# Who issues the small transfers: rotary swaps and key copies move from ScalarE's DMA queue to SyncE's

## The chip, the cores and the metric

The kernel runs on one core of one Trainium2 chip. The metric is device time in microseconds (us), from a median of three runs. A core has a matrix engine (TensorE, PE in the profile), two elementwise engines (VectorE, DVE; ScalarE, ACT), GpSimd (POOL) and SyncE (SP), which computes nothing and only issues transfers. ScalarE can issue transfers too. Every engine works through its own instructions strictly in order: an instruction that waits holds back everything written behind it on that engine.

## What is computed

Two layers of a decoder trunk on 512 tokens of width 1024. The change is in layer 0, the attention layer; the rest (two squared-ReLU MLPs and an RWKV-7 layer) is untouched. Cut to what matters:

```python
proj = h @ w_in                      # one combined projection: aq, ak, av, bq, bk, bv
def partial_rope(t, pos):            # rotates the first 16 of each head's 64 dims
    t1, t2 = tf[..., :8], tf[..., 8:16]
    return concatenate([t1*cos - t2*sin, t2*cos + t1*sin, tf[..., 16:]])
oa = mixture_of_dilations(partial_rope(aq)*scale, partial_rope(ak), av)          # 8 heads
ob = differential_attention(partial_rope(bq)*scale, partial_rope(bk), bv, lam)   # 4 heads, two maps each
return concatenate([oa, ob]) @ w_out
```

## The kernel before

All data are float32; a product is made of three matmuls on float32r halves: a tile x is split into a high part (a cast on ScalarE) and a low part (x minus the high part, on VectorE). Weights come in chunks of 256 rows by 512 columns, 512 KB each: one transfer issued by SyncE into `wraw` (three buffers), the cast `whi` on ScalarE (line 179), the rest `wlo` on VectorE (line 181). One chunk costs TensorE 24 matmuls.

`gemm_stream` (line 226) runs five projections one behind another, four chunks each: Qa (queries of the first mixer), Qka (its keys), Qb, Qkb (the same of the second mixer), Vb; then the output projection. All five share four PSUM banks. In the last chunk of a Q or K projection each bank is finished in turn, and `evac` (line 489) empties it: ScalarE copies it to `qraw` (line 493, two buffers), VectorE multiplies it by cos (line 494), and four small transfers of 8 partitions by 512 elements build the swapped rows in `sw` (lines 496 and 497, three buffers); GpSimd multiplies `sw` by sin into `rt` (line 499), and three pieces of the stream later VectorE adds `rt` (line 500). The next projection's first matmul into a bank waits until line 494 has read it. A third `qraw` waits until the transfers of the first have landed.

Beside the stream runs the attention itself. `stacked` (line 505) prepares one pair of heads: `qs` on ScalarE and VectorE, `kh` on ScalarE, `kl` on VectorE, each for one half of the partitions; two transfers of 64 by 512 elements copy `kh` and `kl` to the other half (lines 515 and 517). For each block of 128 queries TensorE makes scores, VectorE adds the mask (line 535), ScalarE takes the exponential (line 538), TensorE transposes it, ScalarE copies the transpose to `pts` (line 547), and TensorE multiplies it by V into `o`. So `pts` stands on ScalarE in the same line as the weight casts, the `qraw` copies and, before the change, the issues of the small transfers.

The order of the attention steps and the stream's pieces is written out by slots (`FILL`, line 112) and is fixed on TensorE: each TensorE instruction is bound behind the one before it. On the other engines a scheduler sets the order when the program is built; transfers are instructions of their issuing engine there.

Of the kernel before, what the change touches and what calls it, by code (L numbers as in the profile page):

```python
# [10 lines left out]
F32 = mybir.dt.float32  # L11
# [145 lines left out]
class Builder:  # L157
# [252 lines left out]
    def attention_layer(self):  # L410
        tc, nc, A = self.tc, self.nc, self.A
        with ExitStack() as ctx:
# [73 lines left out]
            def project_qk(c0, name):  # L486
                q = [ac.tile([P, S], F32, tag=f"Q{name}{m}", name=self.nm("Q" + name)) for m in range(4)]

                def evac(m, ps):
                    raw = aw.tile([P, S], F32, tag="qraw", name=self.nm("qraw"), bufs=2)  # L490
                    sw = swp[state["sw"] % 3]
                    state["sw"] += 1
                    nc.scalar.copy(raw, ps)
                    nc.vector.tensor_tensor(q[m], ps, cos, op=ALU.mult)  # L494
                    for o in (0, HD):
                        nc.scalar.dma_start(sw[o:o + 8], raw[o + 8:o + 16])
                        nc.scalar.dma_start(sw[o + 8:o + 16], raw[o:o + 8])
                    t = aw.tile([P, S], F32, tag="rt", name=self.nm("rt"))
                    nc.gpsimd.tensor_tensor(t, sw, sin, op=ALU.mult)
                    soon.append((count["pieces"] + 3, lambda: nc.vector.tensor_tensor(q[m], q[m], t, op=ALU.add)))  # L500
                return q, dict(w=W, row0=0, nk=KT, c0=c0, x=(xh, xl), evac=evac)
# [3 lines left out]
            def stacked(q, k):  # L505


                maps = []
                for hh in range(2):
                    own, other = SIDES[hh], SIDES[1 - hh]  # L510
                    qs, kh, kl = (aw.tile([P, S], F32R, tag=f"{n}{hh}", name=self.nm(n)) for n in ("qs", "kh", "kl"))
                    nc.scalar.activation(qs[own], q[own], AF.Copy, scale=-0.125)
                    nc.vector.scalar_tensor_tensor(qs[other], q[own], -0.125, qs[own], op0=ALU.mult, op1=ALU.subtract)
                    nc.scalar.copy(kh[own], k[own])
                    nc.scalar.dma_start(kh[other].bitcast(F32), kh[own].bitcast(F32))
                    nc.vector.tensor_tensor(kl[own], k[own], kh[own], op=ALU.subtract)
                    nc.scalar.dma_start(kl[other].bitcast(F32), kl[own].bitcast(F32))
                    maps.append((qs, kh, kl))
                return maps

# [84 lines left out]
            def steps_a(q, k, v, oh, ol, slot0):  # L605
                for m in range(4):
                    u = {}

                    def prepare(m=m):
                        prepared["a", m] = stacked(q[m], k[m])  # L610
# [29 lines left out]
            def steps_b(q, k, v, oh, ol, slot0):  # L640
                for h in range(4):
                    u, first = {}, slot0 + 4 * h

                    def prepare(h=h):
                        prepared["b", h] = stacked(q[h], k[h])
# [66 lines left out]
            plain, nc = nc, InOrder(self, ["tensor"])  # L712
# [25 lines left out]
            nc = self.nc = plain  # L738
# [1011 lines left out]
```

## Time and profile before

| | before |
|---|---|
| median of 3 runs (lowest, highest) | 1522.94 us (1520.53, 1524.39) |
| the profiled execution's own time | 1522.35 us |
| its span, first to last instruction | 1520.5 us |
| TensorE busy | 1427.7 us (94%) |
| VectorE busy | 889.8 us (59%) |
| ScalarE busy | 701.7 us (46%) |
| GpSimd busy | 351.6 us (23%) |
| mean granted TensorE clock | 0.972 |
| DMA queue of SyncE (q1): packets, MB | 103240, 140.37 |
| DMA queue of ScalarE (q10): packets, MB | 16320, 22.03 |

Times in the rows below count from the span's start. Issuing a transfer is not counted as busy time of an engine; it stands in the trace as a row of its own (ACTq, SPq), and its duration is how long that engine's instruction stream was held, not how long the data took. A number in square brackets at a row's end is how long the engine stood idle before it, and what released it. The granted clock is given as a share of full speed: 1.00 is 2.4 GHz, 0.50 is 1.2 GHz. The attention layer ends about 284 us into the span.

### The profile page before, as it was taken

How to read it: one execution, taken by the hardware profiler on the slowest of the kernel's cores; microseconds unless marked ns; L12 is line 12 of the kernel's file. 1: busy time of each engine (PE TensorE's matmuls, PEld its weight loads, DVE VectorE, ACT ScalarE, POOL GpSimd, SP SyncE). 2: the span in 40 equal slices, each digit the busy share in tenths (PEclk: the TensorE clock that was granted, in tenths of full speed). 3: DMA queues.
4: the chain of work that ended last, by engine and by line, in shares of the span. 5: the costliest groups of instructions: out<-in, count | busy, mean ns of one | idle time of the engine just before them, and what ended most of it. 6: DMA issues, size and time to landing. Idle time of an engine off the chain costs nothing. (4 is left out here: it accounts for less than half of the span.)

```text
span 1520.5 us, 24493 instructions
## 1 busy us (share of the span) xinstructions
PE 1427.7 (94%) x9506; PEld 1180.4 (78%) x9506; DVE 889.8 (59%) x1531; ACT 701.7 (46%) x1426; POOL 351.6 (23%) x368
## 2 busy tenths in 40 slices
PE   8988899999999999979888999989999999999998
PEld 6776687878888888857667788867787888888887
DVE  5545568833335464497866778878866333454543
ACT  4335576532234343336634666666655233343533
POOL 5111100300000010052345455546655000000100
PEclk9999999999999999979989999989999999999999
DMA  5242222333333343225554445444224333323331
GB/s 198 77 118 81 58 79 77 82 97 97 96 97 97 97 125 97 100 56 167 172 193 138 118 137 161 123 140 119 65 95 125 85 97 97 96 97 97 97 97 70
DMA packets 119676, 163.97 MB, mean 108 GB/s; under 512 B 23036, under 2 KB 58404, under 8 KB 119560
## 3 DMA queue, kind: packets, MB, share of 16 engines
q1 hardware_dynamic: 103240, 140.37, 31.0%
q10 hardware_dynamic: 16320, 22.03, 4.5%
q8 instruction: 75, 1.23, 0.3%
q14 instruction: 41, 0.34, 0.1%
HBM read 133.00 MB, written 19.92 MB: 101 GB/s over the span
## 5 line engine op out<-in xcount | busy, mean ns | idle before, releaser
L181 DVE TENSOR_TENSOR wlo<-wraw,whi 128x1024 fp32r<-128x1024 f32 x172 | 221.0, 1285 | 245.0 <-ACT whi L179 244.9
L179 ACT CAST whi<-wraw 128x1024 fp32r<-128x1024 f32 x172 | 180.2, 1048 | 225.9 <-PE g L189 185.0
L190 PE MATMUL g<-xh,wlo 128*128 128x512 f32 x512 | 199.1, 390 | 0.7 <-DVE wlo L181 0.6
L188 PE MATMUL g<-xh,whi 128*128 128x512 f32 x512 | 199.4, 390 | 0.0
L189 PE MATMUL g<-xl,whi 128*128 128x512 f32 x512 | 199.3, 389 | 0.0
L188 PE MATMUL g<-mh,whi 128*128 128x512 f32 x512 | 199.2, 389 | 0.0
L189 PE MATMUL g<-ml,whi 128*128 128x512 f32 x512 | 199.2, 389 | 0.0
L190 PE MATMUL g<-mh,wlo 128*128 128x512 f32 x512 | 199.2, 389 | 0.0
L366 POOL TENSOR_TENSOR acc<-acc,sq 128x512 f32<-128x512 f32 x29 | 49.4, 1705 | 610.5 <-issue 436.6
L196 DVE TENSOR_TENSOR ml<-m,mh 128x512 fp32r<-128x512 f32 x128 | 87.9, 689 | 151.2 <-ACT mh L195 151.2
L195 ACT CAST mh<-m 128x512 fp32r<-128x512 f32 x128 | 78.8, 617 | 190.2 <-PE g L190 190.0
L190 PEld LDWEIGHTS g<-xh,wlo 128*128 128x128 f32 x512 | 96.1, 188 | 21.4 <-DVE wlo L181 1.6
L188 PEld LDWEIGHTS g<-mh,whi 128*128 128x128 f32 x512 | 96.1, 188 | 20.1
L189 PEld LDWEIGHTS g<-xl,whi 128*128 128x128 f32 x512 | 96.1, 188 | 19.8
L188 PEld LDWEIGHTS g<-xh,whi 128*128 128x128 f32 x512 | 96.1, 188 | 19.9 <-ACT rb L372 0.2
L189 PEld LDWEIGHTS g<-ml,whi 128*128 128x128 f32 x512 | 96.1, 188 | 19.9
L190 PEld LDWEIGHTS g<-mh,wlo 128*128 128x128 f32 x512 | 96.1, 188 | 19.9
L149 POOL TENSOR_TENSOR wlo<-wraw,whi 128x256 fp32r<-128x256 f32 x100 | 76.2, 765 | 122.7 <-ACT whi L149 119.7
L806 POOL TENSOR_TENSOR xl<-mt,xh 128x512 fp32r<-128x512 f32 x28 | 50.1, 1803 | 84.0 <-ACT xh L804 77.4
L149 PE MATMUL side<-whi,xh 128*128 128x256 f32 x192 | 63.4, 330 | 0.0
L149 PE MATMUL g<-xh,whi 128*128 128x512 f32 x128 | 52.3, 409 | 8.2 <-DVE Qka L494 4.4
L188 PE MATMUL g<-whi,xh 128*128 128x512 f32 x128 | 51.6, 418 | 6.0 <-ACT xh L804 4.7
(331 smaller groups left out, 3079.8 us busy)
## 6 DMA issues: line engine op xcount, KB each, us to landing
wraw<-in_mlp_w_dram SPq DMA_DIRECT2D x128, 512.0 KB
wraw<-in_attn_w_in_dram SPq DMA_DIRECT2D x24, 512.0 KB
wraw<-in_rwkv_w_o_dram SPq DMA_DIRECT2D x16, 512.0 KB
wraw<-in_attn_w_out_dram SPq DMA_DIRECT2D x8, 512.0 KB
wraw<-in_rwkv_w_k_dram SPq DMA_DIRECT2D x8, 512.0 KB
wraw<-in_rwkv_w_r_dram SPq DMA_DIRECT2D x8, 512.0 KB
wraw<-in_rwkv_w_v_dram SPq DMA_DIRECT2D x8, 512.0 KB
xt<-in_x_dram ACTq DMA_DIRECT2D x4, 512.0 KB
```

The source lines that it names most:

```text
L149: ins = op(*args, **kw)
L179: ins = [nc.scalar.copy(hi, raw)]
L181: ins.append((eng or nc.vector).tensor_tensor(lo, raw, hi, op=ALU.subtract))
L188: mm(ps, lh, rh, start=start, stop=False)
L189: mm(ps, lh, rl, start=False, stop=False)
L190: mm(ps, ll, rh, start=False, stop=stop)
L195: nc.scalar.copy(hi, src)
L196: nc.vector.tensor_tensor(lo, src, hi, op=ALU.subtract)
L366: nc.gpsimd.tensor_tensor(self.acc[0], self.acc[0], sq, op=ALU.add)
L806: eng.tensor_tensor(xl[k], t, xh[k], op=ALU.subtract)
```

## The change

All four swap transfers of each rotary evacuation (16 evacuations, 64 transfers) and both copies in each half of `stacked` (32 transfers) are issued by SyncE. Nothing else in the source changes: no tile, no buffer count, no slot.

```diff
                     nc.vector.tensor_tensor(q[m], ps, cos, op=ALU.mult)
                     for o in (0, HD):
-                        nc.scalar.dma_start(sw[o:o + 8], raw[o + 8:o + 16])
-                        nc.scalar.dma_start(sw[o + 8:o + 16], raw[o:o + 8])
+                        nc.sync.dma_start(sw[o:o + 8], raw[o + 8:o + 16])
+                        nc.sync.dma_start(sw[o + 8:o + 16], raw[o:o + 8])
...
                     nc.scalar.copy(kh[own], k[own])
-                    nc.scalar.dma_start(kh[other].bitcast(F32), kh[own].bitcast(F32))
+                    nc.sync.dma_start(kh[other].bitcast(F32), kh[own].bitcast(F32))
                     nc.vector.tensor_tensor(kl[own], k[own], kh[own], op=ALU.subtract)
-                    nc.scalar.dma_start(kl[other].bitcast(F32), kl[own].bitcast(F32))
+                    nc.sync.dma_start(kl[other].bitcast(F32), kl[own].bitcast(F32))
```

TensorE's and GpSimd's order stays as it was, row for row; ScalarE's, VectorE's and SyncE's change. Three places:

ScalarE, the last evacuation of Qb (`qraw_1060`); minus is before, plus is now, and the numbers behind the names tell tiles apart:

```order
 L538 ACTIVATE sb_1050,sums_887<-sb_1050,mn_1051 128x256
+L179 CAST whi_1072<-wraw_1070 128x1024
+L547 COPY pts_1093<-t_1091 128x128
 L493 COPY qraw_1060<-g_793 128x512
-L179 CAST whi_1072<-wraw_1070 128x1024
-L496 DMA sw_419<-qraw_1060 8x512
-L497 DMA sw_419<-qraw_1060 8x512
-L496 DMA sw_419<-qraw_1060 8x512
-L497 DMA sw_419<-qraw_1060 8x512
-L547 COPY pts_1093<-t_1091 128x128
 L538 ACTIVATE sb_1098,sums_887<-sb_1098,mn_1099 128x384
```

The copy `pts_1093` stood behind the `qraw` copy, a cast and four issues; now it stands ahead of that `qraw` copy, behind the cast alone.

ScalarE, the last evacuation of Qkb (`qraw_1487`) up to the next `pts` that TensorE wants (`pts_1562`), before:

```order
L493 COPY qraw_1487<-g_1079 128x512
L538 ACTIVATE sb_1505,sums_1378<-sb_1505,mn_1506 128x512
L496 DMA sw_417<-qraw_1487 8x512
L497 DMA sw_417<-qraw_1487 8x512
L496 DMA sw_417<-qraw_1487 8x512
L497 DMA sw_417<-qraw_1487 8x512
L179 CAST whi_1511<-wraw_1509 128x1024
L195 CAST oh_814<-oc_1526 128x512
L547 COPY pts_1562<-t_1558 128x384
```

and now:

```order
L179 CAST whi_1511<-wraw_1509 128x1024
L493 COPY qraw_1471<-g_1078 128x512
L547 COPY pts_1500<-t_1497 128x256
L538 ACTIVATE sb_1505,sums_1378<-sb_1505,mn_1506 128x512
L512 ACTIVATE qs_1798<-Qb_442 64x512
L195 CAST oh_814<-oc_1526 128x512
L514 CAST kh_1799<-Qkb_446 64x512
L493 COPY qraw_1487<-g_1079 128x512
L547 COPY pts_1562<-t_1558 128x384
```

The issues are gone from in front of `pts_1562`; the `qs` and `kh` of the next head pair, which stood behind it, have moved ahead of it, and the weight cast `whi_1511` ahead of the third `qraw` copy.

SyncE, the end of the train of Qka's swaps (sixteen rows, of which the last two stand here) and what is now queued behind it; before, the two weight loads followed directly on the one ahead of the train:

```order
+L496 DMA sw_418<-qraw_774 8x512
+L497 DMA sw_418<-qraw_774 8x512
+L515 DMA kh_822<-kh_822 64x512
+L517 DMA kl_823<-kl_823 64x512
+L515 DMA kh_831<-kh_831 64x512
+L517 DMA kl_832<-kl_832 64x512
 L177 DMA wraw_875<-in_attn_w_in_dram 128x2x512
 L177 DMA wraw_931<-in_attn_w_in_dram 128x2x512
```

The weight loads `wraw_875` (Qb's last chunk) and `wraw_931` now wait behind sixteen swaps and four copies. At Qa's train the load `wraw_685` stands behind sixteen swaps in the same way; at Qb's and Qkb's the next loads do too.

## Rows read from the trace of the kernel before

**Rows 1.** Who TensorE waited for, first 430 us: total, times, longest, us

```profile
PE o L149 <- ACT pts L547: 10.1, 5, 4.6
PE g L149 <- DVE Qka L494: 4.4, 2, 2.4
PE g L149 <- DVE Qa L494: 3.7, 2, 2.0
```

**Rows 2.** Stretches: length, busy us (count) by engine, granted clock, DMA share, GB/s

```profile
60.00:80.00 20.00, 16.25 (x60) 12.19 (x59) 14.90 (x14) 7.22 (x10) 5.15 (x4) 0.83 0.25 69
80.00:100.00 20.00, 15.60 (x68) 12.26 (x67) 7.79 (x11) 5.22 (x8) 4.69 (x3) 1.00 0.34 99
120.00:140.00 20.00, 15.84 (x109) 11.81 (x108) 11.14 (x23) 11.01 (x25) 4.30 (x3) 0.83 0.24 61
160.00:185.00 25.00, 19.63 (x134) 15.14 (x133) 11.36 (x24) 10.37 (x26) 5.81 (x4) 0.86 0.24 67
```

**Rows 3.** Timeline of TensorE, the longest stall at Qb and two at Qkb: start, us

```profile
128.04 0.48 PE L149 MATMUL o<-Va,pts 128*64 128x64 f32 x4 [3.78 <-ACT pts L547]
...
162.75 0.69 PE L149 MATMUL o<-Va,pts 128*64 128x64 f32 x16 [0.76 <-ACT pts L547]
...
175.85 0.91 PE L149 MATMUL o<-Va,pts 128*64 128x64 f32 x12 [4.61 <-ACT pts L547]
```

**Rows 4.** Timeline of ScalarE, end of Qb's and of Qkb's last swap issues

```profile
127.04 0.63 ACTq L497 DMA_DIRECT2D sw<-qraw  x1
127.72 0.27 ACT L547 COPY pts<-t 128x128 f32<-128x128 f32 x1 [1.81 <-issue]
...
173.89 1.04 ACT L179 CAST whi<-wraw 128x1024 fp32r<-128x1024 f32 x1 [2.03 <-issue]
...
175.32 0.48 ACT L547 COPY pts<-t 128x384 f32<-128x384 f32 x1
```

**Rows 5.** Stretches of the evacuations of Qb and of Qkb, columns as in Rows 2

```profile
112.50:128.10 15.60, 10.88 (x88) 8.12 (x87) 8.71 (x17) 6.44 (x18) 3.83 (x3) 0.98 0.19 51
158.60:175.90 17.30, 11.93 (x94) 9.10 (x93) 8.54 (x18) 7.17 (x17) 4.39 (x4) 0.98 0.24 62
```

**Rows 6.** Timeline of ScalarE and VectorE at Qa's evacuation

```profile
67.74 0.58 ACT L493 COPY qraw<-g 128x512 f32<-128x512 f32 x1 [2.54 <-issue]
...
61.70 2.23 DVE L181 TENSOR_TENSOR wlo<-wraw,whi 128x1024 fp32r<-128x1024 f32 x1 [0.26 <-ACT whi L179]
...
64.46 0.68 DVE L494 TENSOR_TENSOR Qa<-g,cos 128x512 f32<-128x512 f32 x1
```

**Rows 7.** Timeline at Qka: ScalarE's first swap issue, VectorE's third and fourth cos product

```profile
85.47 0.63 ACTq L496 DMA_DIRECT2D sw<-qraw  x1
...
92.78 0.68 DVE L494 TENSOR_TENSOR Qka<-g,cos 128x512 f32<-128x512 f32 x1
...
96.89 0.69 DVE L494 TENSOR_TENSOR Qka<-g,cos 128x512 f32<-128x512 f32 x1
```

**Rows 8.** Issues by line: duration ns min/median/max, first and last start

```profile
L496 ACTq DMA_DIRECT2D sw<-qraw x32: 631/632/1260, 56.8 to 172.6; - x32
L515 ACTq DMA_DIRECT2D kh<-kh x16: 468/468/553, 95.8 to 240.5; - x16
L1125 SPq DMA_DIRECT2D kb<-kt x16: 472/483/1117, 794.5 to 1086.5; - x16
```

**Rows 9.** Weight loads: issues of SyncE, one load's DMA share, casts on ScalarE

```profile
75.00 0.37 SPq L177 DMA_DIRECT2D wraw<-in_attn_w_in_dram  x1
...
78.00:79.00 1.00, 1.00 (x6) 0.81 (x5) 0.14 (x1) 0.83 (x1) 0.00 (x0) 1.00 0.13 47
...
80.11 5.81 SPq L177 DMA_DIRECT2D wraw<-in_attn_w_in_dram  x2
...
110.94 1.05 ACT L179 CAST whi<-wraw 128x1024 fp32r<-128x1024 f32 x1 [0.55 <-PE g L149]
```

**Rows 10.** Timeline of GpSimd, the first product with the swapped rows

```profile
61.55 1.29 POOL L499 TENSOR_TENSOR rt<-sw,sin 128x512 f32<-128x512 f32 x1 [27.97 <-DVE Qa L494]
```

## The prediction

> **What bounds the kernel now.** TensorE is busy 94% of the span, so I first asked where it is not, and who ends that idle time. The view of who waited for whom, cut to the first 430 us and to TensorE, names three rows that matter here [rows 1]: 10.1 us in five waits for `pts` copies of ScalarE, 4.4 us in two waits for the cos product of Qka, 3.7 us in two waits for that of Qa. Together 18.2 us. The table by stretches places them: TensorE is busy 16.25, 15.60 and 15.84 of 20 us in the stretches from 60, 80 and 120 us, and 19.63 of 25 us from 160 [rows 2]. These are the last chunks of Qa, Qka, Qb and Qkb, the four times when banks are evacuated and swaps are issued. I call them places 1 to 4.
>
> The same table shows a second cost. The granted clock is 0.83 from 60 to 80, 0.83 from 120 to 140 and 0.86 from 160 to 185 [rows 2]. A mean of 0.83 over 20 us is 6.8 us at half speed (1.2 instead of 2.4 GHz), that is 3.4 us of lost work; place 4 loses 25 x 0.14 = 3.5 us. Place 2 stalls for 4.4 us in two pieces and keeps a clock of 1.00 [rows 1, 2], so not each stall pays it.
>
> Then the timelines. TensorE's two longest waits are 3.78 us, ended at 128.04, and 4.61 us, ended at 175.85, both by `pts` [rows 3]. On ScalarE the copy at 127.72 starts as soon as the last of four swap issues, 127.04 + 0.63, is over; ScalarE stood idle 1.81 us for "issue". At place 4 the weight cast follows at 173.89 after 2.03 us of "issue", and `pts` only at 175.32 [rows 4]. From 112.5 to 128.1 ScalarE computes 6.44 us of 15.6, from 158.6 to 175.9 it computes 7.17 of 17.3 [rows 5]: it is not short of time to compute, its stream is held by issuing. That is the wait which ends last at places 3 and 4.
>
> At places 1 and 2 it is a mixture: the wait is for VectorE's cos product, which follows ScalarE's `qraw`. The fourth `qraw` of Qa starts at 67.74 after 2.54 us of "issue", but the third cos product (64.46) follows VectorE's own work, among it a weight low part that took 2.23 us from 61.70 [rows 6].
>
> **The change part by part.** *What it removes from ScalarE.* 64 swap issues of 0.632 us and 32 copy issues of 0.468 us [rows 8]: 40.4 + 15.0 = 55 us of held instruction stream. Only the part that ends a wait of TensorE counts, so the sum is made by place, out of the waits and the clock.
>
> *Place 3.* Its waits for `pts` are the 10.1 us less place 4's 4.61 and 0.76 [rows 1, 3]: 4.7 us, of which 3.78 in one. In the new order four issues are gone from in front of each `pts`; `pts_1093` has one cast ahead of it instead of a copy, a cast and four issues. Four issues are 4 x 0.63 and gaps, 2.7 us, and the issues of the tiles before had delayed ScalarE already. With 6.44 us of computing in 15.6 [rows 5] each `pts` should be ready before TensorE, with 10.88 us of work, asks. Gain between 2.7 (one tile's issues alone) and 4.7; I take 4.3.
>
> *Place 4.* Waits of 4.61 and 0.76 [rows 3], 5.4 us. Here the new order is less kind: ahead of `pts_1562` now stand `qs` and `kh` of the next heads, and the `kh` cast needs the first Qkb tile with its `rt` added, hence its swaps landed. The two that moved ahead cost ScalarE about 1.2 us (half-tile operations, about 0.6 each, as the whole-tile copy in Rows 6), and TensorE asks at 175.85 - 4.61 = 171.24, some 12 us after the first of those swaps. I expect a residue of 0.6 us. Gain between 2.7 and 5.4; I take 4.8.
>
> *Places 1 and 2.* VectorE's order up to the third cos product is unchanged, so the first wait at each stays nearly whole. For the fourth, the four issues ahead of `qraw` go, and two half-tile operations each on ScalarE and VectorE come in ahead (`qs` at place 1, `kh` and `kl` at place 2). At place 2 VectorE would go: third cos product until 92.78 + 0.68 [rows 7], two `kl` and one addition at about 0.7 each, fourth cos product at 95.6 instead of 96.89: gain 1.3 us. At place 1 the same count from 64.46 + 0.68 gives 67.3, or 68.7 if the `qs` are stretched as the low part of 2.23 us was; now it follows the copy that ends at 68.32 [rows 6]: between a loss of 0.4 and a gain of 1.0, and I take 0.5.
>
> *The clock.* If the long stalls at places 3 and 4 go, the drops there should go: 3.4 and 3.5 us, less about 0.4 each for idle time that fell inside: 6 us for both. Place 1 keeps a stall of about 2 us, so I leave its clock as it is; its recovery would be worth 2.6 us more (3.4 less half of the second stall).
>
> *What it adds to SyncE.* The trace has no swap issued by SyncE. The nearest row is a transfer inside SBUF of the RWKV layer, `kb`, which SyncE issues in 0.483 us, where ScalarE needs 0.468 for the key copies [rows 8]: the price hardly depends on the engine, so I take 0.63 and 0.04 of gap for a swap; its ends are 0.63 and 1.26, the longest swap issue. SyncE's stream is in order too, and queued behind a swap that waits for its `qraw` are weight loads, for which TensorE would wait. A load lands about 3.6 us after its issue (issued at 75.00, the DMA share is down to 0.13 from 78 to 79) [rows 9]; the cast of 1.05 us [rows 9] and a low part of 1.2 to 2.2 us follow. Place 1: the train starts at 56.8 [rows 8] and goes out as the four copies come, until about 69. `wraw_685` behind it is Qka's last chunk, which TensorE begins some 2 us ahead of Qka's first swap at 85.47 [rows 7], so at about 83; ready by 69 + 3.6 + 2.3 = 75, it has 8 us to spare. Place 2: the train starts at 85.5, the fourth `qraw` comes at about 94, its swaps end at 97, four copies at 0.47 end at 99. `wraw_875`, issued at 85.5 now (the second of the two from 80.11 on [rows 9]), would go out at 99 and be ready by 105 to 107; TensorE turns to it when the chunk ahead of it ends, at 110.94 [rows 9] less the 1.8 us gained so far. It is hidden by 2 us or more. At places 3 and 4 attention is interleaved, a chunk takes longer, and the loads have more. Cost taken: 0; ends 0 and 5 us (at 1.26 us for a swap the train ends 9 us later and `wraw_875` comes up to 5 us late). The key copies' own move gains nothing: none of TensorE's waits in Rows 1 is for them, and their data are used several us later.
>
> A page of the Trainium skill speaks against the change. Perfetto Trace Analysis, section DMA Optimizations, advises balancing transfers over the engines that can issue them where generating descriptors is the bottleneck; the change gathers them on one. By that rule SyncE would be the next to be late, about 1545 as in the second rival; by Rows 8 and 9 its stream has room, 1505.
>
> *The sum.* 0.5 + 1.3 + 4.3 + 4.8 + 6 = 16.9 us. The profiled execution took 1522.35, which gives 1505.4; it lies 0.6 below the median of the three runs, which I neglect. Forecast 1505.
>
> **The rivals.** *Half of it comes back* (1513). One of places 3 and 4 keeps its long wait since the new order on ScalarE puts something that itself waits in front of `pts`: at place 4 `kh`, which waits for swaps, GpSimd and VectorE; at place 3 the cast `whi_1072`, which waits for TensorE's chunk to end. Price: one of the two gains, about 4.5 + 3 = 7.5 us. For it speaks that both stand so in the new order; against it that the swaps' data have some 10 us to arrive.
>
> *SyncE's train is slow* (1545). A swap may hold SyncE not 0.67 us but about 2, as long as one takes to land: the first four issues at Qa begin at 56.8 and end near 60.1 (one of 1.26, three of 0.67), and GpSimd starts on their data at 61.55 [rows 8, 10], 2.1 us after the last began; and in the new order nearly each swap waits for the landing of the transfer eight before. A train then lasts 32 us. At place 1 it ends at 89 and `wraw_685` is ready at 95, 12 us late; at place 2 the same count gives 125, 14 us late, and the `qraw` that wait for landings eat the gains at places 3 and 4: 1522 + 26 = 1548, about 1545 with some gain left. It begins to cost from about 0.95 us for a swap, where place 2's load just gets late, and makes the kernel slower than before from about 1.6. Against it: eight transfers back is 5 us back, and a swap lands in 2.
>
> *Nothing* (1522). What ScalarE spends on issuing is not what holds `pts`, or the same waiting appears on VectorE. Against it: 1.81 and 2.03 us of "issue" right ahead of the two late steps [rows 4]. DMA: Bandwidth & Descriptors of the Trainium skill, section Issuing engines are not separate DMA queues, says that using several engines only saves the sequencer's time to issue, "which is usually small relative to the DMA itself". Were it small here, moving it would change nothing; the trace does not agree, since 2.7 us of issuing for a tile stand against 2.1 us from an issue to its data.
>
> *More* (below 1499). Place 1's stall shrinks under what brings the clock down, since no weight load now runs beside the first swaps: 2.6 us, and the first stalls at places 1 and 2 lose another 1 to 2 us each.
>
> **How the numbers follow.** Forecast 0.58 (1499 to 1510), half back 0.17 (1510 to 1516), more 0.08, nothing 0.09 (1518 to 1527), slow train 0.08. Leaving out "nothing", "slow train" and the far end of "more" (0.03) leaves 0.80: range 1497 to 1517. What a measurement here can tell from no change is 0.3%, 4.6 us: faster 0.58 + 0.17 + 0.08 = 0.83, same 0.09, slower 0.08.
>
> **What would show it.** Right: TensorE's waits for `pts` fall from 10.1 us to under 2; those for Qka fall by about 1, those for Qa hardly; the clock is 1.00 from 100 to 200 us; the attention layer ends about 17 us earlier and nothing else moves beyond the clock's own play. SyncE's swaps last about 0.63 us. Wrong: a wait of `whi` or `wlo` for a load of weights, swap issues on SyncE above 0.95 us, a `pts` that comes after a `kh` or `whi` that waited, or a clock that stays low at places 3 and 4 though their stalls are gone. Clock drops of the layers behind may fall elsewhere when everything ahead is shorter; a few us either way there would be no sign for or against any step.

## The result: 1504.2 us, and the profile after

The changed kernel takes 1504.2 us (median of 4 runs, 1503.35 to 1506.7) against 1523.12 (1520.53 to 1524.39) for the kernel before. The ratio is 0.988, 95% interval 0.986 to 0.990. Forecast was 1505 in a range of 1497 to 1517. The profiled execution took 1504.68 us where before's took 1522.35, 17.7 us less; the spans are 1502.9 and 1520.5.

First the same view as [rows 1], who TensorE waited for in the first 430 us (total, times, longest). Only the rows that matter here are shown:

```profile
PE g L149 <- DVE Qka L494: 3.1, 2, 1.7
PE g L149 <- DVE Qa L494: 2.7, 2, 1.9
PE s L149 <- DVE ol L199: 2.6, 2, 2.2
```

The row for `pts` is gone (10.1 us before); Qka fell from 4.4 to 3.1 and Qa from 3.7 to 2.7. Together 12.4 us less. The table by stretches, columns as in [rows 2]:

```profile
60.00:80.00 20.00, 17.30 (x64) 13.15 (x63) 10.89 (x13) 6.44 (x9) 6.54 (x4) 0.83 0.31 90
...
120.00:140.00 20.00, 20.00 (x153) 15.60 (x152) 13.06 (x27) 12.90 (x30) 3.37 (x3) 1.00 0.44 123
...
160.00:185.00 25.00, 25.00 (x201) 19.67 (x201) 16.30 (x36) 14.57 (x35) 3.16 (x2) 1.00 0.34 98
...
220.00:240.00 20.00, 17.57 (x93) 14.82 (x92) 16.20 (x53) 10.53 (x37) 1.01 (x1) 0.91 0.21 66
```

At places 3 and 4 (now in the stretches from 100 to 185) TensorE is busy all the time at a clock of 1.00. That gives back 20 x 0.17 = 3.4 and 25 x 0.14 = 3.5 us. Place 1 keeps its 0.83. And a low clock turned up in a stretch where before had none: 0.91 from 220 to 240, which costs 20 x 0.09 = 1.8 us. So by these means the clock gave 5.1 us, and with the 12.4 us of waits that is 17.5 of 17.7 us. The agreement is closer than the account deserves: a mean over a stretch also counts low clock while TensorE stands idle, which the waits count already. An estimate that takes, microsecond by microsecond, only the time that TensorE worked at the low level gives back 6.3 us at places 3 and 4 together, less 1.6 for the new drop and 0.5 for place 1: 4.2 us, and 12.4 + 4.2 = 16.6. That fits what the traces show at the last transposes of the attention layer, first before, then now:

```profile
277.43 0.66 PE L149 MATMUL oc<-ident,ob 128*128 128x128 f32 x4 [0.40 <-DVE ob L593]
260.71 0.66 PE L149 MATMUL oc<-ident,ob 128*128 128x128 f32 x4 [0.38 <-DVE ob L593]
```

They come 16.7 us earlier. The other 0.9 us of the span came in the layers behind, which the change does not touch; where, stays open.

Why `pts` no longer comes late is seen on ScalarE. These are the end of Qb's evacuation (place 3) and of Qkb's (place 4), to be held against [rows 4]:

```profile
117.18 1.05 ACT L179 CAST whi<-wraw 128x1024 fp32r<-128x1024 f32 x1
119.01 0.27 ACT L547 COPY pts<-t 128x128 f32<-128x128 f32 x1 [0.78 <-PE t L149]
...
157.25 0.62 ACT L512 ACTIVATE qs<-Qb 64x512 fp32r<-64x512 f32 x1
...
158.24 0.63 ACT L514 CAST kh<-Qkb 64x512 fp32r<-64x512 f32 x1
158.76 0.59 ACT L493 COPY qraw<-g 128x512 f32<-128x512 f32 x1
159.24 0.49 ACT L547 COPY pts<-t 128x384 f32<-128x384 f32 x1
```

The `pts` at 119.01 is `pts_1093`, the one at 159.24 `pts_1562`; before, they started at 127.72 and 175.32, with four issues shortly ahead of them. At 119.01 ScalarE waits 0.78 us for TensorE's transpose, so now ScalarE is the one that is early. At place 4 `qs`, `kh` and the last `qraw` stand in front of `pts` as the new order said, and none of them waited.

SyncE's side, issues by line as in [rows 8] (duration ns min/median/max, first and last start):

```profile
L497 SPq DMA_DIRECT2D sw<-qraw x32: 624/624/1272, 57.2 to 161.4; - x32
...
L515 SPq DMA_DIRECT2D kh<-kh x16: 461/467/588, 96.0 to 216.7; - x16
```

A swap holds SyncE 0.624 us where it held ScalarE 0.632. So the price of issuing did not change; it was moved from an engine with something urgent to do to one without. What queued behind the train at place 2 is seen on SyncE, and the next weight cast and scores on ScalarE and TensorE:

```profile
98.89 1.14 SPq L177 DMA_DIRECT2D wraw<-in_attn_w_in_dram  x2
...
104.53 1.04 ACT L179 CAST whi<-wraw 128x1024 fp32r<-128x1024 f32 x1
...
103.42 0.22 PE L149 MATMUL s<-kh,qs 128*128 128x128 f32 x1
```

The first of the two loads, `wraw_875`, went out at 98.9 us and its cast started at 104.53 without having waited for it; the scores at 103.42 had not waited for the key copies, which went out from 96.0 on.

### The profile page after: what moved, and what is told of

Same layout as the page of the kernel before. It is cut to its first block, busy times and chain, and to the rows that moved or that the text cites. A ratio compares the mean times of both kernels' runs of the same rounds, so it can differ in the third digit from the quotient of the medians.

```text
span 1502.9 us, 24530 instructions
## 1 busy us (share of the span) xinstructions
PE 1421.1 (95%) x9506; PEld 1174.4 (78%) x9506; DVE 890.4 (59%) x1531; ACT 703.0 (47%) x1426; POOL 351.1 (23%) x368
## 5 line engine op out<-in xcount | busy, mean ns | idle before, releaser
L149 PE MATMUL side<-wlo,xh 128*128 128x256 f32 x192 | 55.5, 289 | 1.8 <-POOL wlo L149 1.7
```

The lines of the kernel that those rows point to most:

```text
L149: ins = op(*args, **kw)
```

## Experiments

**Which transfers, and which places.** Four kernels undo the change in part.

Swaps alone on SyncE:

```diff
-                    nc.sync.dma_start(kh[other].bitcast(F32), kh[own].bitcast(F32))
+                    nc.scalar.dma_start(kh[other].bitcast(F32), kh[own].bitcast(F32))
...
-                    nc.sync.dma_start(kl[other].bitcast(F32), kl[own].bitcast(F32))
+                    nc.scalar.dma_start(kl[other].bitcast(F32), kl[own].bitcast(F32))
```

> The rotary swaps alone on SyncE, the key parts' copies back on ScalarE. The theory (the swaps' issues on ScalarE stood in front of pts and qraw; the copies end no wait of TensorE): the time of the changed kernel within 2 us, 1503 to 1506; waits of TensorE for pts stay gone, clock 1.00 from 100 to 200 us. Rival (the copies' issues carry part of the gain, 32 x 0.47 us = 15 us of ScalarE's stream): about 1510 or more, with waits for pts of 2 us or more back at the fourth place, where two copies stand near pts.

Measured: 1502.68 us, ratio to before 0.989 (0.986 to 0.992). The whole gain is there without the copies (0.3 us below the range expected).

Copies alone on SyncE (the swaps' two lines back on `nc.scalar`):

> The key parts' copies alone on SyncE, the swaps back on ScalarE. The theory: 1521 to 1524, as the kernel before, with waits for pts of about 10 us and the clock at 0.83 from 120 to 140 us. Rival (the copies carry part of the gain): 1515 or less, the waits for pts smaller by several us.

Measured: 1520.8 us against 1520.5 in the same comparison, ratio 1.000 (0.9985 to 1.0012). The copies give nothing, as predicted; TensorE's waits for `pts` are 9.9 us.

By place (this is the edit for places 3 and 4; the other run has `"a", "ka"` in it):

```diff
+                    queue = nc.sync if name in ("b", "kb") else nc.scalar
...
-                        nc.sync.dma_start(sw[o:o + 8], raw[o + 8:o + 16])
-                        nc.sync.dma_start(sw[o + 8:o + 16], raw[o:o + 8])
+                        queue.dma_start(sw[o:o + 8], raw[o + 8:o + 16])
+                        queue.dma_start(sw[o + 8:o + 16], raw[o:o + 8])
```

> Swaps of Qb and Qkb (places 3 and 4) on SyncE, those of Qa and Qka (places 1 and 2) on ScalarE; copies on SyncE. The theory: most of the gain, 10.1 us of stalls and 6 us of clock out of 18.9, so 1505 to 1508; waits for pts gone, those for Qa and Qka as in the kernel before (3.7 and 4.4 us). Rival (it is SyncE's long train at places 1 and 2, or what it does to the loads of weights, that shifts everything behind): 1513 or more.

> Swaps of Qa and Qka (places 1 and 2) on SyncE, those of Qb and Qkb (places 3 and 4) on ScalarE; copies on SyncE. The theory: a gain of the 2.3 us by which the stalls at places 1 and 2 shrank, so 1519 to 1522; waits for pts stay at about 10 us with both clock drops behind them. Rival (gain from places 1 and 2): 1515 or less.

Measured: places 3 and 4 alone 1506.51 us, ratio 0.990 (0.988 to 0.992); places 1 and 2 alone 1518.48, ratio 0.9988 (0.9974 to 1.0002). In us that is 14.0 and 2.0, against 17.8 for all swaps in the same comparison; the 2.0 are not clear of no change, and lie 0.5 us outside the range expected. TensorE's waits in the two, first with places 3 and 4 alone:

```profile
PE g L149 <- DVE Qka L494: 4.3, 2, 2.4
PE g L149 <- DVE Qa L494: 3.5, 2, 2.0
```

and with places 1 and 2 alone:

```profile
PE o L149 <- ACT pts L548: 10.4, 5, 4.6
PE g L149 <- DVE Qka L494: 3.1, 2, 1.7
...
PE g L149 <- DVE Qa L494: 2.6, 2, 1.9
```

Each half of the change does to the waits at its own places what the whole change did, and leaves the others as they were. Some four fifths of the gain come from places 3 and 4.

**Is it the issuing that held ScalarE?** The change also gave ScalarE and VectorE another order and sent the data through another queue. So I left the useful swaps on SyncE and put issuing back on ScalarE: four transfers for each evacuation, to a tile nobody reads. The order, though, is not left as it was: the scheduler, given these issues, gave ScalarE's steps at the four places and behind them the order of the kernel with the copies alone on SyncE, which has the swaps on ScalarE.

```diff
+            idle = ac.tile([P, S], F32, name="idle")
...
+                    for o in (0, HD):
+                        z = o + 16 * (state["sw"] % 4)
+                        nc.scalar.dma_start(idle[z:z + 8], raw[o + 8:o + 16])
+                        nc.scalar.dma_start(idle[z + 8:z + 16], raw[o:o + 8])
```

> The changed kernel with four more transfers for each evacuation, issued by ScalarE to a tile that nothing reads (work beyond the computation); the useful swaps stay on SyncE. The theory (ScalarE's held stream, not the order of SyncE's work nor the data's path, is what made pts late): waits for pts of about 10 us are back, with clock drops at places 3 and 4, and the time is 1518 to 1524. Rival (the gain is that swaps' data come by another engine, or the new order of the casts): 1504 to 1508.

Measured: 1523.04 us, ratio to before 1.0013 (1.0001 to 1.0025): the gain is gone to the last us. Who TensorE waited for:

```profile
PE o L149 <- ACT pts L552: 11.3, 5, 4.7
```

What an idle issue costs ScalarE, in the view by line (columns as in [rows 8]):

```profile
L501 ACTq DMA_DIRECT2D idle<-qraw x32: 632/632/1224, 56.6 to 173.5; - x32
```

And the timeline, of ScalarE up to the late `pts` of place 3 and of TensorE at its longest stalls of places 3 and 4:

```profile
129.37 0.63 ACTq L502 DMA_DIRECT2D idle<-qraw  x1
130.04 0.27 ACT L552 COPY pts<-t 128x128 f32<-128x128 f32 x1 [2.07 <-DMA idle<-qraw]
...
130.36 0.34 PE L149 MATMUL o<-Va,pts 128*64 128x64 f32 x4 [3.98 <-ACT pts L552]
...
176.80 0.91 PE L149 MATMUL o<-Va,pts 128*64 128x64 f32 x12 [4.66 <-ACT pts L552]
```

The useful swaps were out by SyncE, and still `pts` came late. The `pts` at 130.04 starts as soon as the last idle issue, 129.37 + 0.63, is over, after ScalarE stood 2.07 us; behind the three other groups of four issues at this place it had stood 2.50, 3.55 and 2.32 us. So the path of the data and the engine that issues the useful swaps are ruled out as the cause; issuing on ScalarE is it, with the order that the scheduler builds for it. The run does not part these two, but its rows speak against the order alone. At place 3 this order puts one more step of 0.56 us, the `qraw` copy, in front of `pts_1093`, against 10.4 us that ScalarE stood behind issues there. At place 4 it puts less in front of `pts_1562` (`qs` and `kh` come behind it), and TensorE waits 4.66 us all the same.

The Trainium skill (DMA: Bandwidth & Descriptors, section Issuing engines are not separate DMA queues) calls the time that it takes the sequencer to initiate a DMA usually small relative to the DMA itself. For these transfers of 16 KB it is not small: 0.63 us an issue, against 2.1 us from an issue to the first use of its data [rows 8, 10].

**How much may SyncE's train grow?** The same four idle transfers, on SyncE (`nc.sync` in the edit above), so that the train at each place has 32 issues:

> The changed kernel with four more transfers for each evacuation, issued by SyncE to a tile that nothing reads (work beyond the computation): a train of 32 instead of 16 issues at each place, about 1.3 us for each useful swap. By the prediction's slow-train rival this is past the 0.95 us at which wraw_875 gets late: expected is a wait of TensorE for the weight parts at place 2 of 3 to 6 us, with 0 to 3.4 us of clock behind it, so 1507 to 1514, still faster than the kernel before. If the train is hidden even so: 1503 to 1506, and no wait for whi or wlo. If transfers that wait for landings hold SyncE as the rival had it: 1525 or more.

Measured: 1521.37 us, ratio to before 1.0008 (0.9996 to 1.0019). I had expected 1507 to 1514 and a late load. The whole gain is gone, and in the main not for that reason. TensorE's longest stall at place 1, SyncE's last issue for the first tile and ScalarE ahead of the stall, and at place 2 the load `wraw_875` with TensorE's wait for it:

```profile
67.02 0.79 PE L149 MATMUL g<-xh,whi 128*128 128x512 f32 x1 [4.14 <-DVE Qa L495]
...
61.62 0.62 SPq L502 DMA_DIRECT2D idle<-qraw  x1
...
64.18 1.28 ACT L517 ACTIVATE qs<-Qa 64x512 fp32r<-64x512 f32 x2 [3.15 <-DVE Qa L505]
65.48 0.58 ACT L494 COPY qraw<-g 128x512 f32<-128x512 f32 x1
...
112.38 1.14 SPq L177 DMA_DIRECT2D wraw<-in_attn_w_in_dram  x2
...
119.14 0.50 PE L149 MATMUL g<-xh,wlo 128*128 128x512 f32 x1 [0.55 <-DVE wlo L181]
```

The third `qraw` starts at 65.48, behind `qs`, which stood 3.15 us for the first tile with its swaps added. In the changed kernel the third `qraw` starts at 60.65 and only the fourth stands behind a `qs`. With two `qraw` buffers the third copy needs the first buffer's transfers landed, the idle ones too, which read it. The last of them was issued at 61.62; with the 2.1 us of [rows 10] it lands at about 63.7 (an estimate). So most of the delay is the buffer's, and `qs`, which the order puts ahead, takes the rest. The waits for Qa and Qka are 5.5 and 7.0 us here, 2.7 and 3.1 in the changed kernel; new are 2.4 us for Qb and 1.0 for Qkb, and the clock is lower (0.74 from 60 to 80 us, 0.85 from 100 to 120). Late weights cost only 2.5 us, in three pieces. `wraw_875` went out 13.5 us later than in the changed kernel (112.38, 98.89), but TensorE came to its chunk 9.4 us later too (117.88, 108.46). Against TensorE the load fell 4.1 us back and was 0.55 us late, so it had some 3.5 us to spare. No key copy was late.

To separate that from what is queued behind the swaps, sixteen idle transfers behind the last swap of each place. The swaps then go out as in the changed kernel, and what stands behind them goes out 10.7 us later.

```diff
+                    if m == 3:
+                        for z in range(0, P, 8):
+                            nc.sync.dma_start(idle[z:z + 8], raw[z:z + 8])
```

> The changed kernel with sixteen more transfers on SyncE behind the last swap of each of the four places, to a tile that nothing reads (work beyond the computation): the swaps go out as in the changed kernel, the loads of weights and the key copies behind them 10.7 us later, as in the run with four more transfers for each evacuation. If that run lost its 17 us to late loads: the same loss, 1515 to 1523, with waits for whi or wlo. If it lost them to swapped data that came late, so that qs and kh held ScalarE in front of qraw: 1503 to 1507. By the loads' own due times: wraw_875 is cast at 104.5 us in the changed kernel and would be there at about 113, some 6 us too late, with up to 3.4 us of clock: 1510 to 1514.

Measured: 1518.17 us, ratio to before 0.9987 (0.9975 to 1.0000). So delaying what follows the swaps costs nearly as much by itself. TensorE's longest stalls at places 1 and 2 beyond those of the changed kernel, and SyncE's loads between the two trains:

```profile
85.95 0.50 PE L149 MATMUL g<-xh,whi 128*128 128x512 f32 x1 [2.04 <-ACT whi L179]
...
115.03 0.47 PE L149 MATMUL s<-kh,qs 128*128 128x128 f32 x1 [5.36 <-DMA kh<-kh]
...
80.92 7.92 SPq L177 DMA_DIRECT2D wraw<-in_attn_w_in_dram  x5
```

The load of place 1, `wraw_685`, was 2.0 us late with 10.7 us of delay, so it had some 8.7 to spare; the prediction had said 8. But the largest wait is for the copy of `kh` at place 2, 5.36 us: the several us that lie between a key copy and its use are fewer than the 10.7 us of delay. No load made TensorE wait at place 2, but this says nothing on `wraw_875`, which the prediction had named as the first to be late: the order built here sends it out as the fifth of the loads from 80.92 on, ahead of place 2's train, where in the changed kernel it stands behind it. Most of the rest of the loss is clock, 0.91 from 80 to 100 and 0.87 from 100 to 120 us. The measured time lies in the range given for late loads, but what was late in the main was a copy.

The same with the key copies back on ScalarE, to take them out from behind the train:

> The run with sixteen more transfers behind each place's swaps (to a tile that nothing reads, work beyond the computation), with the key parts' copies back on ScalarE, so that only loads of weights stand behind the long train. If the loss there was mainly the key copies (TensorE waited 5.4 us for kh at place 2, with the clock low behind it): 1507 to 1512, no wait for kh, the 2.5 us for whi and wlo at place 1 unchanged. If the loads are the next to be late there, as the prediction's slow-train rival has it for wraw_875: 1514 to 1519, with a wait for whi or wlo of 3 to 6 us at place 2.

Measured: 1524.38 us, ratio 1.0021 (1.0002 to 1.0040), neither of the two. The wait for `kh` is gone and no load was late at place 2 (`wraw_875` goes out ahead of its train here too), but now one was late at place 3:

```profile
139.92 20.20 SPq L177 DMA_DIRECT2D wraw<-in_attn_w_in_dram  x6
...
143.79 1.04 ACT L179 CAST whi<-wraw 128x1024 fp32r<-128x1024 f32 x1 [8.40 <-DMA wraw<-in_attn_w_in_dram]
...
144.89 0.80 PE L149 MATMUL g<-xh,whi 128*128 128x512 f32 x1 [10.60 <-ACT whi L179]
```

In this kernel one load went out between the trains of places 2 and 3, in the run before it three: the scheduler had put the loads in other places when the copies left SyncE. So this run doesn't isolate the copies. It shows that a load can be the late one as well, by where the order leaves it.

**What is left at places 1 and 2.** 5.8 us of waits for the cos product and place 1's clock. The prediction had put the first wait at each place down to VectorE's order. The first test takes VectorE out of the bank's release: the product reads ScalarE's copy.

```diff
-                    nc.vector.tensor_tensor(q[m], ps, cos, op=ALU.mult)
+                    nc.vector.tensor_tensor(q[m], raw, cos, op=ALU.mult)
```

> The changed kernel with VectorE's cos product reading ScalarE's copy qraw in SBUF instead of the PSUM bank, so that a bank is free after the copy alone. The theory (what is left at places 1 and 2 is VectorE's product as the last reader of a bank): the waits for Qa and Qka, 5.8 us, fall to about 1, and the clock drop at place 1 goes (2.6 to 3.4 us), so 1496 to 1500. Rival (VectorE late means qraw is held longer, and with two buffers the third copy waits for the second product, so the same wait comes back by way of ScalarE): 1502 to 1507, with TensorE waiting for qraw.

Measured: 1501.49 us, ratio to before 0.987 (0.985 to 0.9885); the interval overlaps the changed kernel's. Of the 5.8 us 3.8 are left, under another name, and the time lies between the two ranges. The view of waits, then ScalarE and TensorE at place 1:

```profile
PE g L149 <- ACT qraw L493: 3.8, 2, 1.9
...
64.50 1.28 ACT L512 ACTIVATE qs<-Qa 64x512 fp32r<-64x512 f32 x2 [2.60 <-DVE Qa L500]
65.81 0.59 ACT L493 COPY qraw<-g 128x512 f32<-128x512 f32 x1
...
66.45 0.50 PE L149 MATMUL g<-xh,whi 128*128 128x512 f32 x1 [1.90 <-ACT qraw L493]
```

One wait is left at each place, and both are for the fourth `qraw`, which stands on ScalarE behind `qs` (at place 2 behind `kh`), and that waits for swapped data. The first wait at each place, for the third bank, is gone: it was VectorE's product, as the prediction said. Without it TensorE comes to the fourth bank earlier, and waits there for ScalarE. If that order comes from the two buffers, a third should change it; first alone (with the product reading the bank as in the changed kernel):

```diff
-                    raw = aw.tile([P, S], F32, tag="qraw", name=self.nm("qraw"), bufs=2)
+                    raw = aw.tile([P, S], F32, tag="qraw", name=self.nm("qraw"), bufs=3)
```

> The changed kernel with three buffers for qraw; the cos product reads the PSUM bank as before. Theory A (what is left at places 1 and 2 is VectorE's product, last reader of the bank): the waits for Qa and Qka keep most of their 5.8 us, 1502 to 1506. Theory B (with two buffers the third and fourth qraw stand on ScalarE behind a weight cast and the qs or kh casts, which wait for swapped data; a third buffer lets them go ahead): the waits fall to about 1 to 2 us, the clock at place 1 is 1.00 from 60 to 80 us, 1496 to 1500.

Measured: 1498.35 us, ratio 0.985 (0.983 to 0.988). The timeline of ScalarE and TensorE at place 1:

```profile
59.07 0.59 ACT L493 COPY qraw<-g 128x512 f32<-128x512 f32 x1 [0.77 <-PE g L149]
...
61.24 0.59 ACT L493 COPY qraw<-g 128x512 f32<-128x512 f32 x1
64.43 1.28 ACT L512 ACTIVATE qs<-Qa 64x512 fp32r<-64x512 f32 x2 [2.60 <-DVE Qa L500]
...
65.05 0.50 PE L149 MATMUL g<-xh,whi 128*128 128x512 f32 x1 [0.58 <-DVE Qa L494]
```

The stretch of place 1, columns as in [rows 2]:

```profile
60.00:80.00 20.00, 19.42 (x86) 15.76 (x85) 13.81 (x15) 7.90 (x10) 6.55 (x4) 1.00 0.37 116
```

The third and fourth `qraw` (59.07 and 61.24) stand ahead of the `qs` that waits, the stalls at places 1 and 2 are 0.58 and 0.31 us, and the clock at place 1 is 1.00. Theory B of the expectation holds by the waits; by the time alone it is not shown to beat the changed kernel, since the two intervals overlap. VectorE's order changed with it: the third cos product, which stood behind a weight low part and started at 63.71 in the changed kernel, stands ahead of that part now and starts at 59.69. Both edits together:

> As the run before it with three buffers for qraw: the fourth copy waits for the first product and its swaps alone. The theory: 1495 to 1500, places 1 and 2 without a wait over 1 us. Rival (the stalls there are not VectorE's, but come from ScalarE's own casts of weights): no better than the changed kernel, 1502 to 1507.

Measured: 1495.36 us (1493.69 to 1500.55), ratio to before 0.983 (0.981 to 0.986). This beats the changed kernel, whose interval lies wholly above, by some 7 us (0.9834 against 0.9881). Its row for place 1 shows TensorE busy 20.00 of 20 us:

```profile
60.00:80.00 20.00, 20.00 (x90) 16.57 (x89) 14.92 (x15) 8.18 (x11) 7.31 (x4) 1.00 0.37 118
```

And the same two edits on the kernel before, with all issues on ScalarE:

> The kernel before (all issues on ScalarE) with the cos product from qraw and three buffers for qraw. If these two edits cure places 1 and 2 whoever issues the swaps: a gain of 6 to 11 us with the waits for pts still at about 10 us, 1509 to 1515. If the issues in front of each qraw keep ScalarE late there: waits for qraw in place of those for Qa and Qka, 1518 to 1523.

Measured: 1517.68 us, ratio 0.998 (0.997 to 0.9996).

```profile
PE o L149 <- ACT pts L547: 10.8, 5, 5.4
PE g L149 <- ACT qraw L493: 5.0, 2, 2.9
```

The two edits together do little while a `qraw` has issues ahead of it: TensorE's waits in this kernel (above) are for `pts`, as before, and for `qraw` in place of the cos products. The second of the expected cases holds in this, and the time lies 0.3 us below its range. With the swaps on SyncE the two edits are worth more. The third buffer alone on the kernel before was not run.

## Why the prediction was right, and where it was not

**The stalls at places 3 and 4** (4.3 and 4.8 us predicted): 4.7 and 5.4, all of it. The residue of 0.6 us expected at place 4 did not come, since `kh`, which I feared in front of `pts`, did not wait. The ends of the terms were 2.7 and 4.7 or 5.4, and the truth lay at the upper end of both. The run with idle issues on ScalarE shows the cause that the prediction gave, as far as issuing and the order built for it can be told apart.

**Places 1 and 2** (0.5 and 1.3): 1.0 and 1.3. The sizes held, and most of the gain lies where it was put, in the second wait of each place. The prediction took the first wait as fixed by VectorE's own order. It is VectorE's, as the run with the product from `qraw` shows by removing it, but it is not fixed: with a third `qraw` buffer both waits of each place are nearly gone (0.58 and 0.31 us of 5.8 are left). That is the gain of the "more" rival, by a door that the prediction had not seen: it had hoped for the stall to shrink by chance, and place 1's clock with it.

**The clock** (6 us): the two drops went, as predicted, worth 6.3 us by the work done at the low level. A new low stretch at 225 us took 1.6 back and place 1 half a microsecond, which makes 4.2. The term is off by some 2 us for these two; the prediction had allowed a few us for drops that fall elsewhere, and had not put them into the sum. That the sum came out within 1 us of the time is in part luck: the stalls gave 1.5 us more than their terms, the clock 1.8 less, and 0.9 came in the layers behind.

**SyncE's cost** (0, ends 0 and 5): 0, since no wait for `whi`, `wlo` or a key copy is new; a swap takes 0.624 us on it, 0.63 had been taken. `wraw_875` went out at 98.9, the prediction said 99. TensorE came to its chunk at 108.46, and the low part was ready at 106.83: some 2 us of reserve, as predicted. The step was right for the train as it is.

**The rival of the slow train** did not occur, since a swap holds SyncE no longer than it held ScalarE. Its working held in part. It named one late load, `wraw_875`, from 0.95 us a swap on, and a kernel slower than before from about 1.6. In the run with 32 issues, about 1.3 us for a useful swap, that load was indeed the one late passenger at place 2. With its 3.5 us to spare it gets late from 0.67 + 3.5/16 = 0.9 us a swap (an estimate). The copy of `kh` comes next: by the run with sixteen issues behind the swaps it has 10.7 - 5.4 = 5.3 us to spare, 0.33 us for each of 16 issues, so it gets late from 1.0 us a swap (an estimate too); the prediction had given the copies no price. What the working missed is that a longer train also holds the `qraw` buffers. So the gain was gone at 1.3 us a swap already, and of the added waits some 10 us were for the cos products and only 2.5 for weights.

By these estimates the train as it is has room for about a third as many issues again (0.9 against 0.67 us); no run has tried a train between 16 and 32. The Trainium skill (Perfetto Trace Analysis, section DMA Optimizations) says that balancing DMAs over the engines that can issue them may help where descriptor generation is the bottleneck. At this length of train the measured time speaks against it: with half of the swaps back on ScalarE the kernel takes 1506.51 or 1518.48 us, with all of them on SyncE 1502.68. At twice the length no run shows a gain from it: 32 issues on SyncE took 1521.37 us, 16 on each engine 1523.04, and the intervals overlap.

**The rival "half of it comes back"** did not occur: neither the `whi` in front of `pts_1093` nor the `kh` in front of `pts_1562` waited. **"Nothing"** is ruled out by the measured time, and the waits did not come back on VectorE.

## What to carry to other kernels

A transfer costs its issuing engine a piece of its stream that does not grow with what it moves; here it was 0.63 us for a swap of 16 KB, 0.47 for a key copy of 128 KB and 0.37 for a weight load of 512 KB [rows 8, 9]. Count issues times their duration in front of each step that somebody waits for, and give them to an engine whose queue holds nothing urgent, after asking what in that queue now goes out later. Then look at what had hidden behind the wait that you removed; here a third buffer was worth another 4 us by the ratios (not clear of noise), and some 7 with the product read from the copy, where the two edits gave 2.6 us on the kernel before. A scheduler makes each such edit a change of order on three engines. A run that puts back only the cost (idle issues, to a tile nobody reads) rules out more than one that undoes the edit, but it too comes with an order of its own: compare that order before you call the cost alone the cause.

## What the runs showed of the hardware that was not expected

The granted clock does not follow the length of a stall in a simple way. At place 1 the changed kernel stalls 1.93 and 0.77 us and the clock from 60 to 80 is 0.83. With the swaps alone on SyncE it stalls 1.92 and 1.47 us there, and the clock is 1.00; the drop came at place 2 instead, with stalls of 1.93 and 1.28 us (0.83 from 80 to 100). In both kernels the level fell between the two stalls (in the changed kernel the microsecond from 65 to 66 has a mean of 0.58, and the second stall began at 66.8; with the swaps alone 0.56 from 92 to 93, and 92.7), so the second did not bring it. The first was 1.93 us long in both, and 1.92 where the clock stayed at 1.00. The stretches of that run:

```profile
60.00:80.00 20.00, 16.61 (x72) 13.09 (x71) 11.82 (x13) 6.84 (x9) 6.72 (x4) 1.00 0.38 107
80.00:100.00 20.00, 16.80 (x62) 12.89 (x61) 11.72 (x14) 7.97 (x11) 6.45 (x4) 0.83 0.32 79
```

and TensorE's timeline:

```profile
65.05 0.50 PE L149 MATMUL g<-xh,whi 128*128 128x512 f32 x1 [1.92 <-DVE Qa L494]
68.17 0.50 PE L149 MATMUL g<-xh,whi 128*128 128x512 f32 x1 [1.47 <-DVE Qa L494]
...
90.81 0.50 PE L149 MATMUL g<-xh,whi 128*128 128x512 f32 x1 [1.93 <-DVE Qka L494]
```

Likewise the wait for `ol` at 225 us, 2.16 us in the changed kernel with a clock of 0.91 from 220 to 240: with the copies alone on SyncE, and with the product read from `qraw`, it lasted 2.16 us too, at 1.00. What decides between two such stalls stays open here; a term of clock in a sum is right only to within one drop, some 1.6 to 3.5 us.

The issuing time of a transfer was the same on both engines to within 2%: 0.624 and 0.632 us for a swap, 0.467 and 0.468 for a key copy.
